# Modulation loads on ScalarE's queue, nine modulation steps among the GLA branch units, and one subtraction moved in the folded turns

## The chip, the cores and the metric

The kernel runs on one core of a Trainium2 chip. It is one program, launched once. The metric is the device time of that launch in microseconds (us). Before the change three runs gave 2028.0, 2022.18 and 2028.58 us, a median of 2028.0 us. The profile shows one more execution of the same program.

The core has five instruction streams that run side by side, each in order: TensorE (PE in the profile, its weight loads PEld), VectorE (DVE), ScalarE (ACT), GpSimd (POOL) and SyncE (SP). SP, ACT and POOL can start DMA transfers; the instruction that starts one stands in that engine's own order and waits there until the transfer's buffer is free.

## The reference, cut to what matters

One layer of a diffusion backbone is computed for 128 context tokens and 256 latent tokens (384 in all), with 2048 channels, in float32. The change touches three places of it: the modulation (`mod`), the GLA and Fourier branches, and their merge.

```python
mod = silu(cond) @ w_ada + b_ada             # 2048 -> 6 x 2048, one row for context, one for latent tokens
sh1, sc1, ga1, sh2, sc2, ga2 = split(mod, 6)
h = rmsnorm(x, norm_pre_mix) * (1 + sc1) + sh1
proj = h @ w_in                              # q, k, v, GLA output gate g, decay factors, Fourier groups fo
o = gla(q, k, v, decays)                     # two directions, chunks of 64
o = rmsnorm_per_head(o) * gla_out_norm * silu(g)
f = fft2(fo).real                            # over positions and the 256 channels of each of four groups
g_a, g_b = split(sigmoid(h @ w_gate + b_gate))
merged = g_a * (o @ w_br_gla) + g_b * (f @ w_br_four)
m = merged @ w_out
x = x + ga1 * rmsnorm(m, norm_post_mix)
h = rmsnorm(x, norm_pre_ffn) * (1 + sc2) + sh2
x = x + ga2 * rmsnorm((silu(h @ w_ffn_gate) * (h @ w_ffn_up)) @ w_ffn_down, norm_post_ffn)
```

The first two of the six modulation vectors are needed at once and are computed at the start. The other four are needed late, and their work is spread in small steps over the stages between. The change is about these steps.

## The kernel before

**Weights and products.** Activations lie with channels on the 128 partitions and the 384 tokens along the free dimension, 16 tiles of 128 channels (`KT`). Every weight passes as a granule of 128 x 1024 float32 (512 KB): SP loads it into `raw`, ACT casts it to the high part `whi` (L275), DVE subtracts to get the low part `wlo` (L278), and PE multiplies three times (high x high, high x low, low x high), 24 matmuls of 128 x 384 for each granule (`gemm`, L317). `take()` hands out the oldest finished granule, `push()` loads and splits one more, and `grab()` does both; so at each `grab()` the granule that is split is the one three places further on. `whi` and `wlo` have four buffers.

Three kinds of granule differ. Those of the Fourier columns of `w_in` are folded across before they are split (`fold_across`, DVE at L248 and L249, ACT at L251); their high part is cast at once (L283) and their low part (L284) is put into the list `low_due`, which the next `split` empties first. Those of `w_br_four` are folded into a buffer `ws` (`fold`, L236 and L237, one buffer). With `hold=True` the low part of such a granule is done only at `settle()`.

**The order of the stages around the change** (times of the profile's execution):
- up to about 450 us: norm, value projection, q and k projections, 25 gate units, the GLA scans;
- about 450 to 546 us: the last seven gate units, two halves each, which makes 14 turns. After each half `run_after` works through a list written out in `after`: `ends` n (sums and differences of two tiles of h, DVE L711 to L717, then ACT casts their high part, L725), `parts` n (the low part of these, `over_parts`, DVE L723) and `f` h, n (`across_n`: sixteen matmuls at L1021 and L1022 of one folded granule with them). In turns 3 to 8 a turn holds all three, in the order `parts`, `f`, `ends`;
- 546 to 717 us: the eight gate units of GLA, o0 to o7 (`proj` with `gcol`), two halves each, and behind each of o2 to o7 two Fourier units (`four`). `gcol` of a unit is held in `later` and runs in the next half, or at the `catch_up` that opens `four`;
- 717 to about 820 us: the sixteen units `a` of the GLA branch, with four more Fourier units behind a1, a4, a7 and a9. Each ends with products and sums on DVE (L1252, L1253), from which `merged` is split;
- about 820 to 965 us: `w_out`, sixteen units of two halves;
- the rest: the feed-forward part.

**The modulation steps.** Five halves of modulation vectors go through `ada_rest`, one generator `ada`: for each of sixteen k a load of 512 KB into `adaw` (two buffers, POOL L676) and two DVE instructions (L679 or L681) that multiply it by silu(cond) and add it to `adacc`; after the sixteenth a bare step, then sixteen small matmuls (L689), then transposes and a few small DVE operations (`ada_tail`). A call of `next(ada)` makes one step. `paced` thins the calls by `rate`, which is 1.0 up to the branch units and 0.88 in `w_out`. Behind unit 12 of `w_out` whatever is left is run at one stroke (`for _ in ada_gen: pass`).

A sixth half goes through `ada_gemv` (`summed`): sixteen steps k0 to k15, one in each half of o0 to o7, each a load of 512 KB into the same two `adaw` buffers (POOL L700) and eight matmuls of 128 x 256 on PE (L702). The step stands behind the half's `gemm`, in `proj`'s `step(side)`.

**The order of the queues.** For PE, ACT, DVE and POOL the order of the instructions is the program's own; only SP's is arranged by the framework. POOL's own work in the stretch is little: the loads above, and the store of each Fourier unit's result, which waits for DVE:

```python
DVE.tensor_mul(y, y, g)
POOL.dma_start(four_d[i], y)
settle()
```

So a modulation load that POOL issues after a Fourier unit stands behind that unit's store, and one that ACT would issue stands behind ACT's work up to the same point of the program.

Of the kernel before, what the change touches and what calls it, by code (L numbers as in the profile page):

```python
# [22 lines left out]
KT = D // P  # L23
# [84 lines left out]
def tile_step(ctx: ExitStack, tc: tile.TileContext, a, o):  # L108
    nc = tc.nc
    PE, ACT, DVE, POOL, SP = nc.tensor, nc.scalar, nc.vector, nc.gpsimd, nc.sync  # L110
# [107 lines left out]
    def load(raw=None):  # L218
        n, src = next(srcs, (0, None))
        if src is not None:  # L220
            spare = spare_raws.pop() if raw is None and spare_raws else None
            if spare:
                raw = spare.tile([P, G], F32, tag="raw3", name="raw3", bufs=2)
            elif raw is None:
                raw = wp.tile([P, G], F32, tag="raw", name="raw", bufs=2)
            dst = raw if len(src.shape) == 2 else raw.rearrange("p (n x) -> p n x", n=src.shape[1])
            SP.dma_start(dst, src)
            raws.append((raw, 1 if n in folded else 2 if n in across else 0, spare))
# [12 lines left out]
    low_due = []  # L241
# [52 lines left out]
    def push(at=None, eng=DVE, hold=False):  # L294
        if not depth[0]:
            load()
        while len(raws) < depth[0]:
            load()
        split(at, eng, hold)

    def take():
        return ready.pop(0)
# [96 lines left out]
    with ExitStack() as s:  # L399
# [139 lines left out]
        for kb in range(KT):  # L539
# [9 lines left out]
            todo = []  # L549
# [145 lines left out]
    def ada_gemv(m, half):  # L695

        pr = pss.tile([P, 256], F32, tag="side", name="pr")
        for k in range(KT):
            w = adap.tile([P, 1024], F32, tag="adaw", name="adaw", bufs=2)
            POOL.dma_start(w, a["w_ada"][m - 2, half, k])  # L700
            for j in range(4):
                PE.matmul(  # L702
                    pr[32 * j : 32 * j + 32, :], spad[:, k, :], w[:, j * 256 : (j + 1) * 256],
                    start=k == 0, stop=k == KT - 1,
                )
            yield
        yield from ada_tail(pr, m, half)

    def over_ends(k, t, r):

        DVE.tensor_add(t, *(x[:, k : k + 2, :].bitcast(F32) for x in hT))  # L711
        ACT.copy(r[:, :, 0 : HC + 1 : HC], t[:, :, 0 : TC + 1 : TC])
        for lo, n, e in ((0, TC, 0), (TC, TL, HC)):
            h, o = n // 2, HT + (0 if lo == 0 else HC - 2)
            hi = lo + n - 1
            DVE.tensor_add(r[:, :, e + 1 : e + 1 + h], t[:, :, lo + 1 : lo + 1 + h], t[:, :, hi : hi - h : -1])
            DVE.tensor_sub(r[:, :, o : o + h - 1], t[:, :, lo + 1 : lo + h], t[:, :, hi : hi - h + 1 : -1])  # L717

    def over_parts(k, r, low):

        hi, lo = (hF[k // 4][:, k % 4 : k % 4 + 2, n, :] for n in range(2))
        if low:
            DVE.tensor_sub(lo, r, hi.bitcast(F32))  # L723
        else:
            ACT.copy(hi, r)  # L725
# [251 lines left out]
    parts = ((0, HT, 0), (HT, T, HT + HL))  # L977
# [17 lines left out]
    with ExitStack() as s:  # L995
        more = s.enter_context(tc.tile_pool(name="more", bufs=1))
        hF = [actp.tile([P, 4, 2, T], F32R, tag=t, name="hF") for t in ("C_lo", "B_hi", "B_lo")]
        hF.append(more.tile([P, 4, 2, T], F32R, tag="hF", name="hF"))
        spare_raws.extend([more] * 2)
        depth[0] = 4  # L1000
        sums, folds = [], {}

        def ends(n):
            t, r = (more.tile([P, 2, T], F32, tag=z, name=z) for z in ("t", "r"))
            over_ends(2 * n, t, r)
            over_parts(2 * n, r, False)
            folds[n] = r

        def across_n(h, n):
            if n == 0:  # L1010
                sums[:] = [pss.tile([P, 2, hi - lo], F32, tag="side", name="pfo") for _ in range(2) for lo, hi, _ in parts]
            w = take()
            push()
            w_of = [x.rearrange("p (g i k c) -> p i k g c", g=2, i=2, k=2) for x in w]
            for k in range(2):
                kt = 2 * n + k
                x = hF[kt // 4][:, kt % 4]
                for g in range(2):
                    for i, (lo, hi, _) in enumerate(parts):
                        p = sums[2 * g + i]  # L1020
                        PE.matmul(p, w_of[0][:, i, k, g, :], x[:, :, lo:hi], start=kt == 0, stop=False)  # L1021
                        PE.matmul(p[:, 0], w_of[1][:, i, k, g, :], x[:, 0, lo:hi], start=False, stop=kt == KT - 1)  # L1022
            if n == 7:
                for g in range(2):
                    X.append(px.tile([P, T], F32, tag="yb", name="X", bufs=4))
                    for i, (lo, hi, _) in enumerate(parts):
                        p = sums[2 * g + i]
                        ACT.copy(X[-1][:, lo:hi], p[:, 1])
                        DVE.tensor_add(X[-1][:, lo:hi], X[-1][:, lo:hi], p[:, 0])

        def run_after():
            for at, todo in enumerate(after):
                for what, *n in todo:
                    if what == "ends":
                        ends(*n)
                    elif what == "parts":
                        over_parts(2 * n[0], folds.pop(n[0]), True)
                    else:
                        if n == [1, 5]:
                            depth[0] = 2  # L1040
                            spare_raws.clear()
                        across_n(*n)
                if at == turns // 2:
                    SP.dma_start(cd, a["consts"][:, C_CE:NC])
                if at >= turns - 3:
                    next(ada, None)
                yield

        ra = run_after()
        for i in range(GF, 32):  # L1050
            proj(psm, hT, gate(more, i), ra)
        catch_up()
        depth[0] = 0
        xq = px.tile([P, HT], F32, name="xq")
        POOL.memset(xq, 0.0)
        qb = pss.tile([P, HT], F32, tag="side", name="pfq")
        for kb in range(0, KT, 4):
            for x_ in range(2):
                for k in range(kb, kb + 4):
                    q = 32 * (k % 4)  # L1060
                    PE.matmul(
                        qb[q : q + 4, :], wq[:, k, :], hF[k // 4][:, k % 4, x_, 0:HT].bitcast(F32),
                        start=kb == 0 and x_ == 0, stop=kb == KT - 4 and x_ == 1,
                    )
        for q in range(0, P, 32):
            ACT.copy(xq[q : q + 4, :], qb[q : q + 4, :])
# [3 lines left out]
    with ExitStack() as s:  # L1070
# [157 lines left out]
        for b, i in mix_order:  # L1228
            if b == "o":
                if i == 1:  # L1230
                    gate_of()
                proj(psm, hT, lambda p, i=i: gcol(p, i), sd)
                if i == 1:
                    gate_of()
                continue
            if b == "b":
                for g in (df, nw):
                    for _ in g:
                        pass
                four(i)  # L1240
            else:
                catch_up()
                if mT is None:
                    mT = alloc_A()
                if i in (0, 3):
                    next(summed, None)
                if KT - 7 <= i < KT - 2:
                    next(ada, None)
                p = psm.tile([P, T], F32, tag="mm", name="pmm")
                gemm(p, grab(hold=True), oT, 8)  # L1250
                g, y = gates.pop((b, i))
                DVE.tensor_mul(g, g, p)  # L1252
                DVE.tensor_add(y, y, g)  # L1253
                settle()
                if late:
                    split_act(*late.pop())
                late.append((mT[0][:, i, :], mT[1][:, i, :], y))
            gate_of()
# [5 lines left out]
    mg32, _ = halves("B")  # L1264
    x1, x1t = halves("C")
    with ExitStack() as s:
# [49 lines left out]
        for i in range(KT):  # L1316
            p = psm.tile([P, T], F32, tag="mm", name="pmm")
            for g in range(2):
                n = 2 * i + g - 2 * KT
                if n < -6:  # L1320
                    w = grab()
                else:

                    w = take()
# [376 lines left out]
        n = 0  # L1701
# [85 lines left out]
        for kind, c, i in steps[:-4]:  # L1787
# [8 lines left out]
            if kind == "D":  # L1796
                w = grab2()
                n, kh = i // 2, i % 2
                if kh == 0:
# [6 lines left out]
                h = hid_last if last_c else hid  # L1806
                todo = [
                    (pd_tiles[t], [[x[:, 2 * kh + m, t * P : (t + 1) * P] for m in range(2)] for x in h], mov_d, kh == 0, kh == 1)
                    for t in range(3)
                ]  # L1810
# [18 lines left out]
            else:  # L1829
                if kind == "A" and i == 0:  # L1830
                    banks(c)
                w = grab2()
# [222 lines left out]
```

## Time and profile before

| | before |
|---|---|
| runs, us | 2028.0, 2022.18, 2028.58 (median 2028.0) |
| profiled execution, us | 2028.91 |
| its span, first to last instruction, us | 2027.0 |
| mean granted TensorE clock | 0.981 |
| PE busy | 1947.3 us, 96% |
| DVE busy | 1637.7 us, 81% |
| ACT busy | 916.0 us, 45% |
| POOL busy | 94.9 us, 5% |
| loads of `adaw` | 96 of 512 KB on POOL, median 4.2 us to landing |
| stores of `four_d` | 16 of 192 KB on POOL, median 3.1 us to landing |

The execution's own time is 1.9 us longer than its span. Matmuls are pipelined and their ends are modelled, so a busy PE is not PE at its peak: what counts is where it sits idle, and for what. A row of the order of time gives the start and the duration in us, the engine, the line, the operation, what it writes and reads, how many instructions are merged into the row, and in brackets the idle time just ahead of it with what ended it. `adaw<-in_w_ada` after the arrow is the landing of a modulation load. A row of the windows gives a stretch of time, its length, the busy time of each engine with its number of instructions, the clock that was granted to TensorE, the share of the DMA engines that was busy, and GB/s.

### The profile page before, as it was taken

The numbers are of one execution on the slowest core, as the hardware profiler recorded it, in microseconds if no ns is written. First come the engines' busy times: TensorE is split into PE (matmuls) and PEld (weight loads), VectorE is DVE, ScalarE is ACT, GpSimd is POOL, SyncE is SP. The second block draws the span as 40 slices with busy tenths as digits, with TensorE's granted clock in tenths as the row PEclk, the third lists the DMA queues.
The fourth block names the chain that finished last, engine by engine and source line by source line (L and its number), as shares of the span: only waits on it lengthen the run. The fifth ranks groups of instructions, "written<-read, shape, count | busy, mean of one in ns | idle before, by whom it ended". The sixth has DMA issues, their size and how long they took to land.

```text
span 2027.0 us, 27593 instructions
## 1 busy us (share of the span) xinstructions
PE 1947.3 (96%) x10566; PEld 1706.6 (84%) x10566; DVE 1637.7 (81%) x2160; ACT 916.0 (45%) x1298; POOL 94.9 (5%) x170
## 2 busy tenths in 40 slices
PE   8999999999986697998999999999999999999998
PEld 6779999998975697998998888888888888888886
DVE  5668888878854467896878988999999889987886
ACT  4235545444443343444645444444444444444445
POOL 0000110110000000010300000000000000000001
PEclk9999999999998898998999999999999999999999
DMA  9975676675654467665526362635454454625244
GB/s 390 381 265 190 236 242 214 228 245 156 225 155 152 157 227 257 211 228 184 192 88 209 120 215 74 218 112 182 126 182 154 133 181 133 195 93 193 74 141 151
DMA packets 199336, 380.54 MB, mean 188 GB/s; under 512 B 14196, under 2 KB 124884, under 8 KB 194852
## 3 DMA queue, kind: packets, MB, share of 16 engines
q1 hardware_dynamic: 179092, 318.68, 46.5%
q0 software_dynamic: 14976, 53.54, 8.6%
q10 hardware_dynamic: 5136, 6.56, 0.9%
q8 instruction: 83, 1.36, 0.3%
q14 instruction: 49, 0.40, 0.1%
HBM read 361.94 MB, written 16.78 MB: 187 GB/s over the span
## 4 chain that ended last, share of the span: by engine, by line
PE 56%; DVE 9%; issue 8%; DMA 2%; ACT 2%; POOL 1%; ACTq 0%; DVEq 0%; POOLq 0%
PE pgu L329 29%; PE pdn L329 17%; PE pmm L317 6%; DVE adacc L681 2%; DVE wlo L278 2%; DMA adaw<-in_w_ada 1%; PE pmm L1472 1%; PE pfo L1021 1%; ACT whi L275 1%; PE ptr L1764 1%; DMA raw<-in_w_out 0%; DMA raw<-in_w_d 0%; POOL four_d L1223 0%; PE pfo L1022 0%; DVE t L711 0%
## 5 line engine op out<-in xcount | busy, mean ns | idle before, releaser
L317 PE MATMUL pmm<-A_hi,whi 128*128 128x384 f32 x1072 | 367.5, 343 | 0.0
L317 PE MATMUL pmm<-A_lo,whi 128*128 128x384 f32 x1072 | 363.6, 339 | 0.0
L317 PE MATMUL pmm<-A_hi,wlo 128*128 128x384 f32 x1072 | 363.1, 339 | 0.0
L1619 ACT CAST whi<-u 128x1024 fp32r<-128x1024 f32 x200 | 210.5, 1053 | 283.5 <-DVE u L1603 86.2
L1619 ACT CAST whi<-raw 128x1024 fp32r<-128x1024 f32 x175 | 184.2, 1053 | 198.5 <-PE pgu L329 60.3
L1630 DVE TENSOR_TENSOR wlo<-u,whi 128x1024 fp32r<-128x1024 f32 x200 | 244.0, 1220 | 32.3 <-ACT whi L1619 17.7
L275 ACT CAST whi<-raw 128x1024 fp32r<-128x1024 f32 x165 | 172.7, 1050 | 176.8 <-DMA raw<-in_w_out 57.0
L329 PE MATMUL pgu<-whi,A_hi 128*128 128x512 f32 x640 | 250.0, 391 | 0.0
L329 PE MATMUL pgu<-whi,A_lo 128*128 128x512 f32 x640 | 249.2, 389 | 0.0
L1630 DVE TENSOR_TENSOR wlo<-raw,whi 128x1024 fp32r<-128x1024 f32 x175 | 213.3, 1219 | 36.8 <-ACT whi L1619 27.2
L278 DVE TENSOR_TENSOR wlo<-raw,whi 128x1024 fp32r<-128x1024 f32 x163 | 198.3, 1221 | 52.7 <-ACT whi L275 51.5
L317 PEld LDWEIGHTS pmm<-A_hi,whi 128*128 128x128 f32 x1072 | 205.4, 192 | 7.0 <-issue 6.1
L317 PEld LDWEIGHTS pmm<-A_lo,whi 128*128 128x128 f32 x1072 | 205.4, 192 | 0.6 <-DVE A_lo L367 0.4
L317 PEld LDWEIGHTS pmm<-A_hi,wlo 128*128 128x128 f32 x1072 | 204.8, 191 | 0.0
L681 DVE SCALAR_TENSOR_TENSOR adacc<-adaw,spad,adacc 128x1024 f32<-128x1024 f32 x150 | 185.7, 1279 | 16.1 <-DMA adaw<-in_w_ada 15.9
L329 PE MATMUL pdn<-whi,hid_hi 128*128 128x512 f32 x480 | 186.9, 389 | 0.0
L329 PE MATMUL pdn<-whi,hid_lo 128*128 128x512 f32 x480 | 186.8, 389 | 0.0
L329 PE MATMUL pgu<-wlo,A_hi 128*128 128x512 f32 x640 | 184.2, 389 | 0.0
L329 PEld LDWEIGHTS pgu<-whi,A_hi 128*128 128x128 f32 x640 | 120.2, 188 | 26.1 <-issue 0.8
L329 PEld LDWEIGHTS pgu<-wlo,A_hi 128*128 128x128 f32 x640 | 120.1, 188 | 25.4
L329 PEld LDWEIGHTS pgu<-whi,A_lo 128*128 128x128 f32 x640 | 120.1, 188 | 25.0
L329 PE MATMUL pgu<-whi,S 128*128 128x512 f32 x480 | 131.1, 395 | 0.0
(406 smaller groups left out, 3051.8 us busy)
## 6 DMA issues: line engine op xcount, KB each, us to landing
adaw<-in_w_ada POOLq DMA_DIRECT2D x96, 512.0 KB, 4.2
raw<-in_w_d SPq DMA_DIRECT2D x88, 512.0 KB, 3.8
slab<-in_w_ada SPq DMA_DIRECT2D x32, 1024.0 KB, 10.5
raw<-in_w_gate SPq DMA_DIRECT2D x64, 512.0 KB, 4.5
raw<-in_w_g SPq DMA_DIRECT2D x48, 512.0 KB, 3.3
raw<-in_w_u SPq DMA_DIRECT2D x48, 512.0 KB, 3.6
raw<-in_w_in SPq DMA_DIRECT2D x44, 512.0 KB, 4.3
u<-in_w_u SPq DMA_DIRECT2D x40, 512.0 KB, 4.7
```

Of the source, the lines that this page charges most:

```text
L275: ACT.copy(hi, raw)
L278: sub = lambda: eng.tensor_sub(lo, raw, hi.bitcast(F32))
L317: PE.matmul(dst, w[wi][:, k * n + n0 : k * n + n0 + P], x[xi][:, k0 + k, :], start=first and k == 0 and j == 0, stop=last and k == kts - 1 ...
L329: PE.matmul(dst, stat[x_][m], mov(w[w_], m), start=first and w_ == m == x_ == 0, stop=last and w_ == m == 1,)
L681: DVE.scalar_tensor_tensor(acc[:, c, :], w, spad[:, k, c : c + 1], acc[:, c, :], op0=ALU.mult, op1=ALU.add,)
L1021: PE.matmul(p, w_of[0][:, i, k, g, :], x[:, :, lo:hi], start=kt == 0, stop=False)
L1472: PE.matmul(hp[u], hw[u][j][:, ((k - 1) % 8) * P : ((k - 1) % 8 + 1) * P], h2[m][:, k - 1, :], start=k == 1 and j == m == 0, stop=k == KT ...
L1619: ACT.copy(hi, src)
L1630: DVE.tensor_sub(lo, src, hi.bitcast(F32))
L1764: PE.transpose(pt[:, j, :], src[:, j * P : (j + 1) * P], ident)
```

## The change

Three edits in one diff.

1. In `ada_gemv` the sixteen loads are issued by ACT and no longer by POOL. Nothing else in the step changes.
2. Among the branch units `next(ada)` is called for i from 5 to 13 and no longer for i from 9 to 13: nine steps in place of five. As the number of steps is fixed, `w_out` has four fewer.
3. In a turn that holds both `parts` and `f`, `over_parts` (the low part of a pair of h's sums) is no longer ahead of `across_n` but inside its first call, behind `push()`, and `low_due` is emptied right behind it. In a turn without `f` it stays where it was. `push()` itself empties `low_due` first, so a folded granule's low part now comes ahead of the low part of h's sums.

```diff
@@ ada_gemv
         for k in range(KT):
             w = adap.tile([P, 1024], F32, tag="adaw", name="adaw", bufs=2)
-            POOL.dma_start(w, a["w_ada"][m - 2, half, k])
+            ACT.dma_start(w, a["w_ada"][m - 2, half, k])
@@ across_n
-        def across_n(h, n):
+        def across_n(h, n, also):
...
             w = take()
             push()
+            if also:
+                over_parts(2 * also[0], folds.pop(also[0]), True)
+                while low_due:
+                    low_due.pop()()
@@ run_after
             for at, todo in enumerate(after):
+                also = [n[0] for what, *n in todo if what == "parts"]
+                if "f" not in [what for what, *_ in todo]:
+                    for n in also:
+                        over_parts(2 * n, folds.pop(n), True)
                 for what, *n in todo:
                     if what == "ends":
                         ends(*n)
-                    elif what == "parts":
-                        over_parts(2 * n[0], folds.pop(n[0]), True)
-                    else:
+                    elif what == "f":
...
-                        across_n(*n)
+                        across_n(*n, also)
@@ the units of mix_order
-                if KT - 7 <= i < KT - 2:
+                if KT - 11 <= i < KT - 2:
                     next(ada, None)
```

## The prediction

> **What bounds the kernel now.** I read the waits first, then the windows that cover the touched stages, then the order of time on each engine inside them. The page gives the span; the waits name the one place where TensorE (PE) stands on a modulation load.
>
> ```profile
> span 2027.0 us, 27593 instructions
> ...
> PE pr L702 <- DMA adaw<-in_w_ada: 40.4, 5, 9.1
> ...
> POOL four_d L1223 <- DVE y L1222: 194.9, 16, 20.3
> ```
>
> The columns of the waits are us in total, times, longest. Five of the sixteen `ada_gemv` steps make PE wait 40.4 us; and POOL, which issues the loads, waits in order for each folded unit's result `y`. The windows (us, busy of PE, PEld, DVE, ACT, POOL with instructions, granted clock, DMA share, GB/s) show the same places:
>
> ```profile
> 546.00:590.00 44.00, 44.00 (x298) 37.94 (x291) 20.70 (x32) 21.68 (x38) 2.65 (x5) 1.00 0.46 147
> 590.00:717.00 127.00, 86.58 (x501) 77.62 (x499) 60.66 (x120) 45.74 (x69) 10.84 (x20) 0.80 0.49 157
> ...
> 822.00:917.00 95.00, 94.90 (x558) 93.72 (x557) 89.89 (x104) 44.55 (x73) 9.55 (x18) 1.00 0.65 219
> 917.00:933.00 16.00, 9.26 (x56) 7.19 (x55) 13.58 (x18) 4.83 (x8) 0.53 (x1) 0.79 0.53 182
> ```
>
> From 546 to 590 (units o0 to o2) PE never waits: POOL has run ahead. From 590 to 717 (o3 to o7) it idles 40 us and its clock falls to 0.80. From 822 to 917 (`w_out`) PE sets the pace, with VectorE (DVE) close behind. Everything from 976 on is untouched.
>
> **Part 1: the sixteen gemv loads on ACT's queue.** Nothing is removed but the place in a queue. On POOL a load stands behind the `four_d` stores; on ScalarE (ACT) it stands behind all of ACT's work up to that step: the cast of `grab`, and `gcol`'s SiLU and `o_hi` cast where `later` holds them. Two groups have to be told apart.
>
> *Units o3 to o7, first half.* One of the five alike:
>
> ```profile
> 605.88 1.08 PE L702 MATMUL pr<-adaw,spad 128*32 128x256 f32 x8 [7.29 <-DMA adaw<-in_w_ada]
> ...
> 599.82 0.55 POOL L1223 DMA_DIRECT2D four_d<-y  x1 [4.00 <-DVE y L1222]
> 600.36 1.07 POOL L700 DMA_DIRECT2D adaw<-in_w_ada  x2
> ...
> 602.02 1.04 ACT L275 CAST whi<-ws 128x1024 fp32r<-128x1024 f32 x1 [3.90 <-DVE ws L237]
> ```
>
> POOL issues at 600.36, as soon as `y` is stored. The cast at 602.02 belongs to `grab()` of this very half; it waits for a fold that DVE does after that same `y`. In ACT's order the load comes behind it, so it goes out between 602.1 (if it leaves while the cast runs, which no row shows) and 603.06 (behind it): 1.7 to 2.7 us later. What counters it is the transfer. From issue to landing (min/median/max), first `raw` from SP in 546 to 590, then `raw` in 590 to 717, then `adaw` from POOL in 590 to 717:
>
> ```profile
> DMA to landing us min/median/max: 3.3/3.6/4.4
> ...
> DMA to landing us min/median/max: 3.5/5.0/7.3
> ...
> DMA to landing us min/median/max: 4.7/6.2/7.1
> ```
>
> With SP's 5.0 the load lands at 607.1 to 608.1, against PE's start at 605.88: each stall grows by 1.2 to 2.2 us. I take 1.7; five make **+8.5** (6 to 11; with the minimum of 3.5 they would be -1.5). The second load of each pair is issued a cast later and has a whole half before its use: nothing.
>
> *Units o0 to o2, six steps.* ACT's last instruction ahead of each load, and the gemv that needs it:
>
> ```profile
> 547.68 1.05 ACT L275 CAST whi<-raw 128x1024 fp32r<-128x1024 f32 x1
> 554.42 1.05 ACT L275 CAST whi<-raw 128x1024 fp32r<-128x1024 f32 x1
> 565.70 0.51 ACT L366 CAST o_hi<-gs 128x384 fp32r<-128x384 f32 x1 [2.30 <-DVE gs L1172]
> 571.20 1.05 ACT L275 CAST whi<-ws 128x1024 fp32r<-128x1024 f32 x1 [1.43 <-DVE ws L237]
> 584.48 0.51 ACT L366 CAST o_hi<-gs 128x384 fp32r<-128x384 f32 x1 [0.68 <-DVE gs L1172]
> 585.33 1.06 ACT L275 CAST whi<-raw 128x1024 fp32r<-128x1024 f32 x1
> ...
> 550.56 0.64 PE L702 MATMUL pr<-adaw,spad 128*32 128x256 f32 x8
> 557.27 0.64 PE L702 MATMUL pr<-adaw,spad 128*32 128x256 f32 x8
> 564.88 0.64 PE L702 MATMUL pr<-adaw,spad 128*32 128x256 f32 x8
> 573.49 0.64 PE L702 MATMUL pr<-adaw,spad 128*32 128x256 f32 x8
> 581.63 0.64 PE L702 MATMUL pr<-adaw,spad 128*32 128x256 f32 x8
> 588.45 0.64 PE L702 MATMUL pr<-adaw,spad 128*32 128x256 f32 x8
> ```
>
> None of these gemvs waits today. ACT's chain in each half hangs on PE matmuls of the same half or the step before it, so the offsets hold when earlier stalls shift both. Issue behind the named instruction and 3.6 us to landing give: k0 548.7+3.6 against 550.5, +1.9; k1 555.5+3.6 against 557.2, +1.9; k2 566.2+3.6 against 564.9, +4.9; k3 572.2+3.6 against 573.4, +2.4; k4 585.0+3.6 against 581.6, +7.0. For k5 ACT no longer carries k4's `gcol`, so I let its cast end about 1.5 us into its half, which gives +0.7. Together 19; with issue while the cast runs about 14.6; with 4.4 to landing 24. I take **+17**.
>
> *The clock.* The same eight gemv matmuls take 1.08 us after a stall and 0.64 without. The clock of 0.80 over 127 us is 25 us lost on five stalls; about half of it falls inside the idle time, which leaves some 2.4 us felt per long stall (an estimate). k2 and k4 are long. Whether the shorter ones count is open: this wait, which ends in the next fence at 458.75, lasted 2.08 us, and its matmul took 0.53 where its like at 467.40 took 0.36. I take **+5** (3 to 10). The Trainium skill, "TensorE: Matmul & The Clock Gate", section "Why this matters for your kernels", draws the line at idle gaps of about 3 us; by that the short stalls would be free and the term 4.8, but the 2.08 us row speaks against so sharp a line.
>
> Part 1: +30.5.
>
> **Part 3, costed next: the order in the folded turns.** In turns 3 to 8 DVE now does fold, `over_parts` low (950 ns), low of the granule, low of the gate granule, `ends`. The change puts `over_parts` behind both lows.
>
> ```profile
> 464.25 0.69 DVE L249 SCALAR_TENSOR_TENSOR raw<-raw 128x512 f32<-128x512 f32 x1
> 464.86 0.95 DVE L723 TENSOR_TENSOR hF<-r,hF 128x768 fp32r<-128x768 f32 x1
> 466.12 1.23 DVE L284 TENSOR_TENSOR wlo<-raw,whi 128x1024 fp32r<-128x1024 f32 x1 [0.31 <-ACT whi L283]
> ...
> 465.03 1.06 ACT L283 CAST whi<-raw 128x1024 fp32r<-128x1024 f32 x1 [0.39 <-DVE raw L249]
> ...
> 458.75 0.53 PE L1022 MATMUL pfo<-hF,wlo 128*128 128x194 f32 x1 [2.08 <-DVE wlo L284]
> 467.40 0.36 PE L1022 MATMUL pfo<-hF,wlo 128*128 128x194 f32 x1 [0.42 <-DVE wlo L284]
> ```
>
> PE does wait for this low part, so the aim is real. But the low part needs ACT's cast, which starts after the fold and ends at 466.09; it cannot start before 466.1 whatever stands ahead of it. `over_parts` fills that hole today. Moved, the hole stays (1.2 us idle) and some 0.9 us comes later, ahead of the next fold, for which PE waits. Six turns give 5.2 if DVE sets the pace alone; in every other turn another ACT cast holds DVE for a while, which takes part of it back (an estimate). I take **+3.5** (0 to 5). The flush of `low_due` after it finds nothing: the split in the same push has emptied the list.
>
> **Part 2: nine steps instead of five among the `a` units.** Four more steps (units a5 to a8): four POOL loads and four pairs of DVE products come forward, and leave `w_out`.
>
> ```profile
> 753.66 0.69 DVE L236 TENSOR_TENSOR ws<-raw 128x512 f32<-128x512 f32 x1
> 775.75 2.48 DVE L681 SCALAR_TENSOR_TENSOR adacc<-adaw,spad,adacc 128x1024 f32<-128x1024 f32 x2 [2.84 <-DMA adaw<-in_w_ada]
> 793.38 2.48 DVE L681 SCALAR_TENSOR_TENSOR adacc<-adaw,spad,adacc 128x1024 f32<-128x1024 f32 x2 [9.42 <-DMA adaw<-in_w_ada]
> 798.44 2.48 DVE L681 SCALAR_TENSOR_TENSOR adacc<-adaw,spad,adacc 128x1024 f32<-128x1024 f32 x2
> ...
> 754.04 0.54 POOL L1223 DMA_DIRECT2D four_d<-y  x1 [14.12 <-DVE y L1222]
> 784.79 1.07 POOL L676 DMA_DIRECT2D adaw<-in_w_ada  x2
> ...
> 797.61 0.66 PE L317 MATMUL pmm<-o_hi,whi 128*128 128x384 f32 x1 [9.06 <-DVE gate L1252]
> 929.46 1.08 PE L689 MATMUL pr<-adacc,selr 128*32 128x256 f32 x8 [6.13 <-DVE adacc L681]
> ```
>
> These loads stay on POOL, behind the stores. The first pair after a folded unit comes in DVE's order right after the `y` that releases the store that releases the load, so DVE waits a whole landing. Today that costs 2.84 and 9.42 us, 12.3 together, and PE then waits for DVE (797.61). Changed, it happens at three units. a5: store 754.04, load 754.6, landing 6.2 later (two loads at once, as in o3 to o7), 760.8, where DVE was free at 753.66: 7.1. a8: the same less the low part of the held granule (1.2): 5.5. a10: 9.4, since the same `xT` loads still meet it. Sum 22.0, 9.7 more. The four pairs add 4 x 2.40 = 9.6. About 3 us of DVE's idle time there is filled. So PE's later units start **+16** late (10 with landings of 4.7 and no meeting at a10; 20 with 7.1).
>
> In return the work in `w_out` ends four steps earlier. Today it isn't done when unit 12 drains the generator: PE waits 6.13 us at 929.46, and the window around it has a clock of 0.79, some 3.4 us more. Changed, the last products come two halves of PE work (8.2 us, at 94.90 us per 558 matmuls) ahead of their matmul, more than the 6.13: **-9.5** (-6 if DVE lags more). The rest of `w_out` is PE's own time, so nothing else is won there.
>
> Part 2: +6.5 (+1 to +14).
>
> **The sum.** 30.5 + 3.5 + 6.5 = +40.5 us. The profiled execution took 2028.91 (span 2027.0), the runs 2028.0 in the median, so 0.9 less: 2068.5, said as **2068 us**.
>
> **The rivals.**
> - *Free of the stores, the loads are early* (faster). If ACT issued each load well before POOL's 600.36, the 40.4 us and about 12 us of clock would go: -52, and with the other terms (17 + 5 of the first six, 3.5, 6.5) -20: 2008. It decides at one point: ACT must pass the cast of 602.02 before 600.36. For it: the 20.3 us POOL waits for one `y`. Against it: the cast's own releaser. 4%.
> - *The loads land as before*: ACT is in time everywhere, part 1 is zero: 2028 + 10 = 2038. The idle ACT of 546 to 590 (21.68 of 44 busy) speaks for it, the `o_hi` rows against. 6%. The Trainium skill, "DMA: Bandwidth & Descriptors", section "Issuing engines are not separate DMA queues", says the issuing engine only changes the sequencer's time; by that rule this is the outcome, and the store waits of the trace are what it leaves out.
> - *Lighter*: issue while casts run, short landings, DVE's slack larger: 3 + 14.6 + 3 + 0 + 1 = 22, 2050. 13%.
> - *Heavier*: every landing at its long end and the short stalls cold too: 11 + 24 + 10 + 5 + 14 = 64, 2092. 12%.
> - *It does nothing*: the terms cancel within 6 us, 2028. 3%.
>
> **How the numbers follow.** The forecast has 62%, with 2050 to 2088 as its own range. The range 2046 to 2092 takes in the lighter and the heavier case and leaves out the first two and the last (13%) and some tails. About 0.3% (6 us) is what a measurement of this kernel can tell from no change; only the first rival is below it, only the last inside: faster 0.04, same 0.03, slower 0.93.
>
> **What would show it.** The gemv of L702 should wait for its load in ten or eleven of sixteen steps, some 65 us instead of 40.4, with k2 and k4 among the longest, and `adaw` issued from ACT about 2 us behind `y`. DVE should wait at L681 three times in the `a` units; the 6.13 us at L689 should be gone; the turns before 510 should be 0.9 us longer each. I am wrong if the gemvs of o0 to o2 run unhindered, or if the five old stalls shrink.

## The result and the profile after

The changed kernel took 2072.7 us in the median of four runs (2070.23 to 2074.76), the kernel before 2026.96 (2022.18 to 2028.58, four runs). The ratio is 1.0229, with a 95% interval of 1.0207 to 1.0251: the change makes the kernel some 46 us slower. The profiled execution of after took 2073.94 us, at a mean granted clock of 0.973 (before 2028.91 and 0.981). Lines of the code below the first edit are four to six higher than before: the gate product L1252 is now L1258, the across products L1021 and L1022 are L1025 and L1026.

The page's span and three rows of the waits of after (us in total, times, longest):

```profile
span 2072.2 us, 27589 instructions
...
POOL four_d L1229 <- DVE y L1228: 280.3, 16, 87.6
...
PE pr L702 <- DMA adaw<-in_w_ada: 59.3, 9, 9.3
...
DVE adacc L681 <- DMA adaw<-in_w_ada: 23.1, 6, 8.4
```

PE now stands 59.3 us on gemv loads (those of `ada_gemv`), in nine steps. The 6.13 us at L689 are gone. POOL waits longer for `y` than before, and now nobody minds: the gemv loads no longer stand behind it. The stretches that answer to those of before, in the windows of after:

```profile
553.00:597.00 44.00, 36.42 (x237) 30.84 (x230) 14.35 (x23) 14.97 (x29) 0.00 (x0) 0.92 0.37 119
597.00:751.00 154.00, 102.31 (x579) 90.29 (x578) 67.54 (x129) 53.51 (x80) 5.41 (x10) 0.79 0.42 142
863.00:961.00 98.00, 97.83 (x572) 96.05 (x570) 90.69 (x108) 45.63 (x76) 7.91 (x15) 1.00 0.62 215
961.00:977.00 16.00, 16.00 (x104) 15.32 (x104) 10.36 (x19) 7.99 (x14) 0.00 (x0) 1.00 0.68 205
```

The first row starts where o0 starts: PE, which never waited there, now idles 7.6 of 44 us, on the loads of k1 to k3. In the second it idles 52 us where it idled 40; 6.35 of these are the wait of k4, which has moved into this stretch. The last two are `w_out`: the hole of 917 to 933 is filled and its clock is back at 1.00.

Where the 45.2 us of the two spans arise, by the start of a PE instruction that marks each stage (order of time on PE; us):

| mark | before | after | grown by |
|---|---|---|---|
| last product of the GLA scans | 430.40 | 432.87 | 2.5 |
| first across product | 456.32 | 458.79 | 0.0 |
| product behind the 14 turns (`pfq`) | 543.45 | 550.96 | 5.0 |
| gemv k15 | 716.38 | 749.52 | 25.6 |
| first product of `w_out` | 812.84 | 863.05 | 17.1 |
| first product behind `w_out` (`prow`) | 963.44 | 1003.87 | -9.8 |
| end of the span | 2027.0 | 2072.2 | 4.8 |

The first 2.5 us lie ahead of every edit. The profiles of the experiments, which change nothing in this part either, reach the same mark between 430.00 and 432.53: it differs from run to run.

**One of the five alike**, in the order of time of after:

```profile
628.28 0.55 POOL L1229 DMA_DIRECT2D four_d<-y  x1 [4.01 <-DVE y L1228]
...
630.48 1.04 ACT L275 CAST whi<-ws 128x1024 fp32r<-128x1024 f32 x1 [3.91 <-DVE ws L237]
630.49 0.84 ACTq L700 DMA_DIRECT2D adaw<-in_w_ada  x2
...
635.74 1.08 PE L702 MATMUL pr<-adaw,spad 128*32 128x256 f32 x8 [8.70 <-DMA adaw<-in_w_ada]
```

The store goes out at 628.28; POOL would have issued the load right behind it, at 628.83. ACT issues it at 630.49, because the cast ahead of it waits for the fold behind `y`. But it goes out as this cast starts, not when it ends. **The first units**, which had no wait:

```profile
565.24 0.64 PE L702 MATMUL pr<-adaw,spad 128*32 128x256 f32 x8 [0.39 <-DMA adaw<-in_w_ada]
577.16 1.08 PE L702 MATMUL pr<-adaw,spad 128*32 128x256 f32 x8 [4.26 <-DMA adaw<-in_w_ada]
591.79 0.64 PE L702 MATMUL pr<-adaw,spad 128*32 128x256 f32 x8 [2.93 <-DMA adaw<-in_w_ada]
606.37 1.08 PE L702 MATMUL pr<-adaw,spad 128*32 128x256 f32 x8 [6.35 <-DMA adaw<-in_w_ada]
```

These are k1 to k4: ACT's work up to each step is now in front of its load. k0 and k5 don't wait. **A folded turn** of after, on ACT and DVE:

```profile
466.58 0.69 DVE L249 SCALAR_TENSOR_TENSOR raw<-raw 128x512 f32<-128x512 f32 x1
...
467.36 1.04 ACT L283 CAST whi<-raw 128x1024 fp32r<-128x1024 f32 x1 [0.40 <-DVE raw L249]
...
468.44 1.22 DVE L284 TENSOR_TENSOR wlo<-raw,whi 128x1024 fp32r<-128x1024 f32 x1 [1.17 <-ACT whi L283]
469.58 1.22 DVE L278 TENSOR_TENSOR wlo<-raw,whi 128x1024 fp32r<-128x1024 f32 x1
470.71 0.95 DVE L723 TENSOR_TENSOR hF<-r,hF 128x768 fp32r<-128x768 f32 x1
```

DVE idles 1.17 us for the cast where it idled 0.31, and `over_parts` comes at the end. The low part starts no sooner behind the fold than it did. **The a units**, the three long waits of DVE:

```profile
795.46 2.48 DVE L681 SCALAR_TENSOR_TENSOR adacc<-adaw,spad,adacc 128x1024 f32<-128x1024 f32 x2 [8.40 <-DMA adaw<-in_w_ada]
...
822.87 2.48 DVE L681 SCALAR_TENSOR_TENSOR adacc<-adaw,spad,adacc 128x1024 f32<-128x1024 f32 x2 [4.98 <-DMA adaw<-in_w_ada]
...
843.66 2.48 DVE L681 SCALAR_TENSOR_TENSOR adacc<-adaw,spad,adacc 128x1024 f32<-128x1024 f32 x2 [7.53 <-DMA adaw<-in_w_ada]
```

### The profile page after: what moved, and what is told of

It is laid out like the page before. It is cut to its first block, busy times and chain, and to the rows that moved or that the text cites. A ratio compares the mean times of both kernels' runs of the same rounds, so it can differ in the third digit from the quotient of the medians.

```text
span 2072.2 us, 27589 instructions
## 1 busy us (share of the span) xinstructions
PE 1960.2 (95%) x10566; PEld 1715.6 (83%) x10566; DVE 1639.0 (79%) x2160; ACT 915.8 (44%) x1298; POOL 86.0 (4%) x154
## 4 chain that ended last, share of the span: by engine, by line
PE 59%; issue 8%; DVE 6%; DMA 2%; ACT 2%; POOL 0%; ACTq 0%; DVEq 0%; POOLq 0%
PE pgu L329 28%; PE pdn L329 17%; PE pmm L317 10%; DMA adaw<-in_w_ada 2%; DVE wlo L278 1%; PE pmm L1478 1%; DVE adacc L681 1%; ACT whi L275 1%; PE pfo L1025 1%; PE ptr L1770 1%; DMA raw<-in_w_d 0%; ACT whi L283 0%; DVE t L711 0%; PE pr L702 0%; DVE raw L249 0%
## 5 line engine op out<-in xcount | busy, mean ns | idle before, releaser
L329 PEld LDWEIGHTS pgu<-whi,A_hi 128*128 128x128 f32 x640 | 120.1, 188 | 26.1 <-issue 0.8
L329 PEld LDWEIGHTS pgu<-whi,A_lo 128*128 128x128 f32 x640 | 120.1, 188 | 25.0
```

What stands on the lines that cost most here:

```text
L329: PE.matmul(dst, stat[x_][m], mov(w[w_], m), start=first and w_ == m == x_ == 0, stop=last and w_ == m == 1,)
```

## The experiments

Stage durations by the same marks, from one profile each (us), and the median of the runs with its ratio to before. "Turns" runs from the first across product to `pfq`, "`w_out`" from its first product to `prow`, and "rest" from there to the end of the span:

| kernel | turns | k0 to k15 | k15 to `w_out` | `w_out` | rest | median | ratio (95%) |
|---|---|---|---|---|---|---|---|
| before | 87.1 | 165.8 | 96.5 | 150.6 | 1063.6 | | |
| after | 92.2 | 191.5 | 113.5 | 140.8 | 1068.3 | 2072.7 | 1.0229 (1.0207 to 1.0251) |
| edit 1 alone | 87.0 | 193.1 | 96.1 | 150.7 | 1066.9 | 2057.2 | 1.0149 (1.0129 to 1.0169) |
| edit 2 alone | 86.9 | 160.7 | 111.5 | 140.8 | 1063.4 | 2033.2 | 1.0036 (1.0025 to 1.0047) |
| edit 3 alone | 92.3 | 160.0 | 94.9 | 150.0 | 1063.6 | 2030.6 | 1.0024 (1.0013 to 1.0034) |
| stores on ACT | 87.5 | 117.9 | 93.8 | 149.0 | 1066.7 | 1981.6 | 0.9779 (0.9763 to 0.9796) |
| one ahead, POOL | 87.6 | 129.0 | 96.0 | 151.9 | 1063.6 | 1993.4 | 0.9827 (0.9813 to 0.9840) |
| one ahead, ACT | 87.1 | 132.1 | 96.3 | 149.8 | 1067.0 | 1998.3 | 0.9853 (0.9840 to 0.9867) |
| stores on ACT, nine steps | 87.1 | 120.1 | 100.5 | 140.8 | 1067.5 | 1982.1 | 0.9777 (0.9762 to 0.9792) |
| low part on POOL | 90.1 | 163.8 | 95.0 | 150.5 | 1063.3 | 2032.2 | 1.0018 (1.0009 to 1.0028) |
| two ahead, POOL | 86.8 | 114.4 | 92.9 | 150.6 | 1063.6 | 1976.9 | 0.9749 (0.9734 to 0.9763) |
| two ahead, steps in o | 87.5 | 128.6 | 86.8 | 140.9 | 1063.9 | 1973.2 | 0.9731 (0.9714 to 0.9747) |
| stores on ACT, steps in o | 87.3 | 126.6 | 98.3 | 140.4 | 1066.9 | 1986.4 | 0.9794 (0.9779 to 0.9808) |
| thirty-two tiny copies | 87.2 | 163.7 | 95.0 | 151.4 | 1078.1 | 2042.8, one run | |

Where nothing in them is changed, k0 to k15 took 160.0 to 165.8 in five profiles, as the landings differ; the profile of before was the longest. A single profile's difference there carries some us of that.

**The three edits, each alone.**

```diff
@@ ada_gemv
-            POOL.dma_start(w, a["w_ada"][m - 2, half, k])
+            ACT.dma_start(w, a["w_ada"][m - 2, half, k])
```

> Only edit 1: the sixteen gemv loads are issued by ACT, everything else as before. Theory (place in the order of an engine): in the trace of after this part is worth 25.6 us, measured between the start of the GLA units and the last gemv, and it needs neither of the other edits, so +23 to +28 (ratio 1.0115 to 1.014), and PE waits at L702 in nine or ten steps for 57 to 62 us in total. Rival (the edits feed one another: the later folded turns of edit 3 make the loads late): under +15, with fewer than eight waits. Rival (ACT's queue as such is slower at moving 512 KB): the median from issue to landing is above the 6.2 us of POOL in 590 to 717.

```diff
@@ the units of mix_order
-                if KT - 7 <= i < KT - 2:
+                if KT - 11 <= i < KT - 2:
```

> Only edit 2: nine modulation steps among the a units, five before. Theory (the loads stand behind the stores of the folded units): the a units end 16 to 18 us later and w_out gives back 9.5 to 10, so +6 to +8 (ratio 1.003 to 1.004); DVE waits three times at L681 for 21 to 24 us, and PE's 6.13 us at L689 are gone. Rival (the 17 us of the a units were loads that ACT's late ones pushed together): the a units lose only the 9.6 us of the four pairs of products, which DVE's idle time takes up in part, and the sum is 0 or below.

The third takes edit 3 as the diff of the change shows it, and nothing else.

> Only edit 3: the low part of h's sums behind the granules' low parts. Theory (it leaves DVE a hole of 1.2 us ahead of the cast's end and puts 0.95 us behind it, in six turns): +4 to +6 (ratio 1.002 to 1.003), and the stretch from the first across product to the products of the Nyquist column takes 92 us in place of 87.1. Rival (the aim holds and the loss in after came from elsewhere): -2 to -4.

Measured by the ratios: +30 us (26 to 34), +7 (5 to 10) and +5 (3 to 7). They add up to 42 against 46 for all three together (42 to 51): no edit needs another for its loss, and the rival that they feed one another falls for each. The stages that grow alone are those that grow in after. PE waits 57.2 us in eight steps in the first (expected 57 to 62 in nine or ten); DVE waits three times among the a units in the second, 18.7 us in all, a little less than expected. ACT's transfers themselves weren't slower: in the five old stalls PE's gemv starts 4.6 to 5.15 us behind the issue from ACT there, and 4.74 to 5.25 in after, against 4.74 to 6.45 behind the issue from POOL in before. The first came out above the theory's 23 to 28, and the table shows where: 27.3 in the GLA units and 3.3 behind `w_out`, of which more below.

**The stores out of the way.** No edit; the store goes to ACT.

```diff
-            POOL.dma_start(four_d[i], y)
+            ACT.dma_start(four_d[i], y)
```

> None of the three edits; instead the stores of the folded units go from POOL to ACT, and the loads stay on POOL. Theory (POOL's loads are late because they stand behind a store that waits for DVE): the five waits at L702 go almost whole, 40.4 us and some 12 us of clock, and DVE's two waits at L681 (12.3 us) with them; ACT stands a little longer at y but had to wait for the fold behind it anyway: 1960 to 1985. Rival (the transfers are slow in this stretch, whoever issues them): the waits stay above 25 us and the time within 8 us of before. Rival (ACT, held at y, brings its casts late): the waits at L702 go, but PE waits as long for whi or wlo, 2015 to 2040.

44 us faster than before. No wait at L702 is left, and the GLA units from o3 on, in the windows of this run:

```profile
590.00:676.00 86.00, 81.48 (x535) 72.42 (x534) 61.08 (x121) 47.20 (x70) 5.49 (x11) 1.00 0.72 232
```

They take 86 us with DMA engines 0.72 busy at 232 GB/s, where before took 127 at 0.49 and 157 (with 34 fewer matmul instructions in its window): the transfers had room. What the prediction named as the cause of the five old stalls is shown.

**The place in the program against the engine.** Each gemv load is issued one step earlier, on POOL (stores left there too) and, as a second kernel, on ACT.

```diff
+        ws = []
         for k in range(KT):
-            w = adap.tile([P, 1024], F32, tag="adaw", name="adaw", bufs=2)
-            POOL.dma_start(w, a["w_ada"][m - 2, half, k])
+            for n in range(len(ws), min(k + 2, KT)):
+                ws.append(adap.tile([P, 1024], F32, tag="adaw", name="adaw", bufs=2))
+                POOL.dma_start(ws[n], a["w_ada"][m - 2, half, n])   # second kernel: ACT
+            w = ws[k]
```

> None of the edits; the gemv loads stay on POOL, and so do the stores, but each load stands one step earlier in the program, so that the load for the first half of o3 to o7 comes ahead of the stores of the folded units in between. Theory (it is the place behind the store that costs, nothing else): the five waits of 40.4 us go as they did with the stores on ACT, k0 to k15 takes about 118 us in place of 166, 1972 to 1985; and the 3.5 us behind the last store, which the three kernels with sixteen more transfers on ACT show, are not there. Rival (moving the stores also won something else, such as earlier stores for the a units): 1995 or more.

> Edit 1 alone (loads on ACT) with each load one step earlier in the program. Theory (what costs in edit 1 is ACT's order, not ACT's queue): a step earlier the loads are in time, and PE waits under 8 us at L702 in place of 57; 1972 to 1990, of which about 3.5 us lie behind the last store, as in the other kernels with sixteen more transfers on ACT. Rival (ACT as the issuing engine costs by itself, by holding its casts while a load's buffer is not free): PE waits for casts in place of loads, 2000 to 2030.

The waits for the gemv load, first on POOL, then on ACT (the line is now L705):

```profile
PE pr L705 <- DMA adaw<-in_w_ada: 12.4, 5, 3.3
```

```profile
PE pr L705 <- DMA adaw<-in_w_ada: 15.5, 5, 3.6
```

They are 34 and 29 us faster than before, and both miss the expected numbers: 1993.4 against 1972 to 1985, and 1998.3 against 1972 to 1990, with 15.5 us of waits against under 8. One step ahead saves only the load of each unit's first half. That of the second half still goes out behind the store (on ACT behind the cast that waits for the fold), and is now late itself. Between the medians of the two kernels lie 4.9 us; in their profiles ACT takes 3.1 us more in the GLA units and 3.4 more behind `w_out`, and 2.1 less in `w_out`. With each load at its old place the same choice of engine had cost 30. And no wait of PE for a cast on ACT is longer than 0.8 us in these stages, where the rival would have PE wait for casts in place of loads. So the loss of edit 1 is ACT's order, as the theory had it.

**Both buffers kept full.** Stores and loads on POOL; from the GLA units on each load is issued as soon as the step two places before its own has used its buffer, for gemvs and DVE's products alike.

```diff
+    def refill(n=1):
+        for src in list(islice(fed[0], n)):
+            ahead.append((src, ada_load(*src)))
...
+        refill(2)        # at the start of ada_gemv; fed lists all loads from there on
...
+            refill()     # behind the matmuls of ada_gemv, and the products of ada_rest
             yield
```

> None of the edits; stores and loads stay on POOL, but from the GLA units on POOL keeps both adaw buffers filled: each load, those of the gemvs and those for DVE's products among the a units and in w_out, is issued as soon as the step two places ahead has used its buffer, ahead of the stores in between. Theory (place in the queue): what the one-step version left, 12.4 us of waits at L705 and DVE's 16.8 us for its loads, goes too, some 11 us in the GLA units and 3 in the a units: 1975 to 1984, with about 5 us behind the last store. Rival (two loads at once slow each other and SP's granules in the GLA units): 1988 or more.

1976.9 us, as expected, and 96 us faster than the changed kernel. The windows from k0 to k15, of the a units, and of `w_out`:

```profile
551.00:666.00 115.00, 114.18 (x764) 101.50 (x764) 71.35 (x136) 62.19 (x98) 12.37 (x23) 1.00 0.65 209
675.00:758.00 83.00, 79.82 (x460) 78.60 (x459) 71.68 (x125) 39.47 (x68) 5.93 (x11) 0.98 0.84 289
758.00:909.00 151.00, 143.23 (x835) 139.19 (x834) 128.32 (x160) 67.83 (x110) 10.05 (x19) 0.97 0.62 208
```

PE is busy 114.18 of 115 us, with an unreduced clock.

**Four steps forward, elsewhere.** First the stores on ACT with edit 2, then four steps behind folded (Fourier) units 3, 5, 7 and 9 in place of edit 2's, on the two-ahead kernel and on the one with the stores on ACT.

```diff
                 four(i)
+                if i in (3, 5, 7, 9):
+                    next(ada, None)
```

> The stores on ACT as in the fourth run, and edit 2 with them. Theory (edit 2 lost because its loads stood behind the stores; w_out's gain of 9.8 us is real): with the stores out of the way the four pairs of products cost the a units 0 to 6 us, so 4 to 10 us faster than the stores on ACT alone: 1972 to 1978. Rival (DVE has no room for the products among the a units, whatever the loads do): the a units lose 10 us or more and the time is 1980 to 1988.

> The version with both buffers kept filled, and four more modulation steps, one behind the second folded unit of o3 to o6 (not among the a units). Theory (w_out's gain of 8 to 10 us is real and what edit 2 lost even with its loads in time was DVE's time among the a units; in the GLA units DVE is busy 61 of 86 us and has room): 5 to 10 us faster than the version without these steps, 1967 to 1976. Rival (the products hold back y and the folds, so PE waits for wlo): no gain, within 3 us of the version without.

> The stores on ACT (fourth run, 1981.6) and the same four more steps in the GLA units in place of edit 2's. Theory: 5 to 10 us faster than the stores on ACT alone, 1971 to 1977, where edit 2's places won nothing. Rival: within 3 us of 1981.6.

None brought its 4 to 10 us surely. `w_out` gave its 8 to 10 us back in every one, and the products cost about as much, or more, where they were put. With edit 2's places and loads in time DVE no longer waits long for a load, but it is the fuller engine. The a units of the stores on ACT, and then with nine steps:

```profile
676.00:762.00 86.00, 80.66 (x458) 79.73 (x458) 72.93 (x126) 40.47 (x69) 2.63 (x5) 0.96 0.81 277
```

```profile
679.00:771.00 92.00, 80.82 (x458) 78.05 (x458) 80.74 (x132) 39.69 (x68) 4.57 (x9) 0.98 0.83 280
```

DVE's 7.8 us more make the stretch 6 us longer. In the GLA units the steps cost 14 us of k0 to k15 on the two-ahead kernel (four gemv loads wait again, 10.4 us, as POOL now waits for DVE to free a buffer), of which 6 come back in the a units. Its 1973.2 is the lowest median, but its interval overlaps that of the kernel without these steps. With the stores on ACT the same steps made it slower, 1986.4 against 1981.6; there PE waits 4.8 us for ACT's casts of folded granules and 3.8 us for gemv loads, which it did not without them.

**The low part of h's sums off DVE.**

```diff
-            DVE.tensor_sub(lo, r, hi.bitcast(F32))    # over_parts, low
+            POOL.tensor_sub(lo, r, hi.bitcast(F32))
```

> None of the edits; the low part of h's sums is computed by POOL in place of DVE, at its old place in the program. Theory (on DVE this subtraction lies in a hole that ends with ACT's cast, so ahead of the low part it costs nothing): taking it off DVE changes the turns by less than 1.5 us in all, and the time stays within 3 us of before. Rival (DVE's sum of work sets the turns, and edit 3 lost for another reason): 0.95 us in each of eight turns come off, 5 to 8 us faster, and the stretch from the first across product to the Nyquist product takes 80 to 82 us in place of 87.1.

4 us slower (2 to 6), a little beyond the theory's 3; the rival's 5 to 8 us faster are excluded. The order of time:

```profile
472.93 2.04 POOL L723 TENSOR_TENSOR hF<-r,hF 128x768 fp32r<-128x768 f32 x1 [5.35 <-ACT hF L725]
473.34 1.05 ACT L283 CAST whi<-raw 128x1024 fp32r<-128x1024 f32 x1 [0.40 <-DVE raw L249]
...
474.43 1.62 DVE L284 TENSOR_TENSOR wlo<-raw,whi 128x1024 fp32r<-128x1024 f32 x1 [1.17 <-ACT whi L283]
```

With 0.95 us less to do, DVE waits 1.17 us for the cast, as in after: on DVE the subtraction had filled that hole. The low part takes 1.60 to 1.62 us in place of 1.22 in six turns, where POOL works beside it; by this count that is 2.4 of the 3.0 us that the turns grew by.

**What lies behind the last store.** Two tiny copies on ACT in each gemv step; no transfer moved.

```diff
+            for _ in range(2):
+                ACT.copy(tiny[:, 1:2], tiny[:, 0:1])
```

> The kernel before with thirty-two copies of one element per partition on ACT, two in each gemv step, and no transfer moved. It asks what lies behind the last store: from its issue to the end of the span it took 4.2 to 5.4 us in the five kernels with ACT's transfers as before and 8.7 to 8.9 us in the five with sixteen more. If the length of ACT's instruction stream sets it: about 8.8 us here too, span about 2030. If the number of ACT's transfers sets it: about 5 us, span about 2027.

Last store and span of edit 1 alone, then of this kernel:

```profile
span 2056.9 us, 27594 instructions
...
2048.06 0.40 ACTq L1920 DMA_DIRECT2D out_yT<-x1b  x1
```

```profile
span 2041.0 us, 27603 instructions
...
2035.95 0.42 ACTq L1924 DMA_DIRECT2D out_yT<-x1b  x1
```

From the issue to the end these are 8.8 and 5.1 us. Over all profiles: 8.7 to 8.9 in the six kernels with sixteen more transfers on ACT, 4.0 to 5.6 in the eight without. The length of ACT's instruction stream is not it; it goes with its transfers, by what means stays open. The time of this single run, 2042.8, isn't read: behind `w_out`, in a part that the edit doesn't touch, PE finished 441 matmuls in 100 us in place of 449, and whether the new tile's place in memory or chance did that wasn't tried.

## Why the prediction was right, point by point

The forecast was 2068 us (2046 to 2092), and 2072.7 came. Its mechanism holds in all three parts, in after and with each edit alone. One assumption in it was off: that a load on ACT cannot leave before the cast ahead of it runs. The sizes:

- **Part 1, +30.5.** Edit 1 alone costs 30 us, but this is made up in another way. (a) The five old stalls went from 40.4 to 45.3 us, +4.9 where 8.5 stood, which is below its range of 6 to 11: the load leaves as the cast starts, the earlier of the two times given. The 40.4 vary too: they are 37.0 to 40.0 in the four other profiles with these loads untouched. (b) k1 to k4 wait 13.9 us, where 17 stood; k0 and k5 do not wait. That is close to the 14.6 which the text gave for issue while the cast runs: the term was mis-sized by taking it between that and issue behind the cast. k0's load left even 1.01 us before its cast began. So nine steps wait, 59.3 us, where ten or eleven and some 65 us were expected. k2 and k4 are the longest of the new waits, but shorter than each of the five old ones. (c) What remains of the 25.6, some 6.8 us, is PE running slower; 5 stood. And 3.3 to 3.5 us at the end were in no term.
- **Part 3, +3.5.** 5.0 in after, 5.1 alone. The hole and the 0.95 us behind it are as described; the part that other casts were to take back was not there. The term was nearly its full 5.2, six turns of 0.87 us.
- **Part 2, +6.5.** The a units +17.1 (16 stood) and `w_out` -9.8 (-9.5 stood). DVE waits 8.40, 4.98 and 7.53 us, 20.9 together, where 7.1, 5.5 and 9.4 made 22.0. With loads in time the four steps still cost 7 us, so of the 15 to 17 some 8 to 10 are late loads, and the rest is products, as the two terms had it.
- **The sum.** 40.5 stood against 45.2 in the spans. Part 1's stage gave 4.9 less, parts 3 and 2 together 2.3 more; the end gave 4.8 and the stretch ahead of the edits 2.5, neither of which stood there. That the total came within 5 us is in part luck, as 4.9 too much met 9.6 that was missing.
- **The rivals.** *Free of the stores* fails at the point named: ACT passes the cast 2.2 us behind the store. What it promised is real, though; it takes the loads ahead of the stores (1976.9), not onto ACT. *The loads land as before* rested on the issuing engine not counting. One step ahead it nearly doesn't: 3.1 us in the GLA units between POOL and ACT. By the Trainium skill's "DMA: Bandwidth & Descriptors", section "Issuing engines are not separate DMA queues", transfers run on the same 16 DMA engines whichever engine starts them, and issuing from several saves only the time that issuing takes. The trace agrees for the transfer: at the old stalls 4.74 to 5.25 us lie between the issue from ACT and PE's start, and 4.74 to 6.45 from POOL. What cost 30 us in the change was the work that stands in front of it in the engine's program.

## What to carry to other kernels

A transfer is as early as the last thing in front of it in its engine's program: before moving it to another engine, write down what stands in front on both, and consider moving it up in the order instead. Work brought forward pays only where the engine that does it has room at that place; a wait removed at the far end isn't won until that is counted. And an instruction that seems to delay another may be filling a wait which the other has anyway: look at its second input.

## What the runs showed of the hardware

- A transfer on ACT does not wait for the end of the cast ahead of it. In after, eight of the sixteen gemv loads stand behind a cast that waits for DVE, and left 0.00 to 0.06 us behind the start of that cast (630.49 against 630.48). The other eight stand behind a cast that waits only for ACT's own earlier work, and left before it began: that of k0 1.01 us before.

```profile
554.19 0.37 ACTq L700 DMA_DIRECT2D adaw<-in_w_ada  x1
554.21 0.96 ACT L1072 COPY xq<-pfq 4x194 f32<-4x194 f32 x3
555.20 1.05 ACT L275 CAST whi<-raw 128x1024 fp32r<-128x1024 f32 x1
```

- The clock after a wait has no sharp line. The window behind the 2.08 us wait of before, and two behind waits of 4.26 and 2.93 us in after:

```profile
458.75:461.00 2.25, 2.25 (x8) 2.25 (x9) 1.54 (x2) 1.15 (x2) 0.00 (x0) 0.50 0.49 133
```

```profile
577.16:579.40 2.24, 2.24 (x11) 0.99 (x12) 0.00 (x0) 0.00 (x0) 0.00 (x0) 0.50 0.00 0
591.79:594.00 2.21, 2.21 (x19) 1.79 (x20) 0.36 (x1) 0.56 (x2) 0.00 (x0) 1.00 0.03 7
```

After 2.08 and 4.26 us it is 0.50, after 2.93 it is 1.00; with edit 3 alone it stayed at 1.00 after 2.06 us at the place of the first. From the folded turns to the end of `w_out`, in all profiles, the clock was 0.50 behind every wait of 3.9 us or more, and went both ways between 2 and 3.6: 0.50 behind 3.05 us in the kernel one ahead on POOL, 1.00 behind 3.40 us in the one on ACT. The Trainium skill, "TensorE: Matmul & The Clock Gate", section "Why this matters for your kernels", has about 3 us; the traces here show no sharp line there.
- Sixteen more transfers on ACT lengthen the end of the program by some 3.5 us, and a POOL subtraction stretches a DVE one from 1.22 to 1.62 us.
